# Looking up chosen key indices by rank: the one-hot table laid out with slots outermost, then ranks, heads innermost

## The chip, the cores and the metric

One Trainium2 chip, one core. The time is that of one execution on the device, in microseconds; of several runs the median counts. Before the change it is 2786.63 us (three runs, 2783.54 to 2786.88).

## The reference, cut to what matters

Two layers over 256 latent tokens and 256 context tokens of width 1024. Each layer ends in a channel mixer with 16384 experts, which are chosen by product keys: per token and head (8 heads), the query's halves are scored against two sets of 128 keys, the best 16 of each set are kept, their 256 pairs are scored by the sum, and the best 16 pairs name the experts.

```python
s = jnp.einsum('thpd,hpnd->thpn', q, keys).astype(jnp.float32)
s_top, i_top = lax.top_k(s, PEER_TOPK)
cand = (s_top[:, :, 0, :, None] + s_top[:, :, 1, None, :]).reshape(...)
cid = (i_top[:, :, 0, :, None] * PEER_NKEYS + i_top[:, :, 1, None, :]).reshape(...)
best, pos = lax.top_k(cand, PEER_TOPK)
eid = jnp.take_along_axis(cid, pos, axis=-1)
```

Layer 0 routes latent and context tokens (512), layer 1 the latent tokens alone (256). What the change touches is the last step: from a position among the candidates to the two key indices of the pair.

## The kernel before, in words

Tokens lie on the 128 partitions, in tiles i = 0, 1 of each stream (a stream is the latent or the context tokens). peer_route goes over the heads n = 0 to 7. TensorE projects the queries of a head (L796 to L798, each weight split into a rounded and a remainder part, the remainder by POOL in L153, `wl`) and scores them against the keys (L807); ACT copies the scores to SBUF (`S`, L809); DVE takes the best 16 by top16, which makes five calls: the eight largest, their indices, their replacement, the next eight, their indices (L715 to L719). Values go to `m`, indices to `ix`, both laid out [token tile, head, half a of the key, rank]. After every fourth head, for each stream, route_heads(r) is called for the heads `hs` of that half r: two streams by two halves in layer 0, one by two in layer 1, six calls in all.

route_heads copies the half's indices to bf16 (`ixb`, ACT, L726), lets POOL build 112 candidate sums per head (L729, L732), and takes the best 16 of them by top16 on DVE (`best`, `pos`). A position is turned into the ranks of its two halves by shifts and masks (L741 to L744, int32), a copy to bf16 by ACT (L746) and a few small operations on DVE (L747 to L753). Then, for each half a, a pass looks up the key index that stands at this rank:

```python
oh = wk([128, 128, 16], "oh", BF16)
nc.vector.tensor_tensor(oh, rk[:, a, :, None].to_broadcast([128, 128, 16]),
                        C["iota16"][:, None, :].to_broadcast([128, 128, 16]), op=OP.is_equal)
```

compares the 128 ranks of a token (2 tiles by 4 heads by 16 slots) with 0 to 15 (L756); two products, one per token tile, put the 16 indices in place of the ones (L760); three adds halve the 16 columns to two (L762: 1024, 512, 256 elements), and a final add of 128 elements writes the index as f32 to `i12` (L764). The gate is a softmax of `best` (L767 to L772). All of this stands on DVE unless another engine is named.

After the routing, slots_T transposes the indices and gates of each token tile on PE (`trp`, L168) into slots (L822 to L824). From them dense_experts builds a dense gate matrix in blocks of 16 tokens: DVE makes one-hot rows and weighs them (L920, L921, L925, L926; 2048 f16 elements each), PE joins them (`g_ps`, L933), ACT copies the result out and a DMA stores it. PE, ACT and POOL meanwhile work ahead on the first experts: ACT rounds the weights (`uh`, L152), POOL makes the remainders (`ul`, L153), PE multiplies (`u_ps`, L885 to L887). Then the main loop over all 128 experts runs, mostly on PE.

The order of instructions in the routing is not written by hand: the program that builds the kernel puts each engine's instructions in an order of its own, fixed before the run, and independent work (top16 of other heads, work ahead on experts) is interleaved with a pass. Only the one-hot blocks and the main loop are held in a written order.

Of the kernel before, what the change touches and what calls it, by code (L numbers as in the profile page):

```python
# [10 lines left out]
BF16 = mybir.dt.bfloat16  # L11
F16 = mybir.dt.float16
I32 = mybir.dt.int32
U32 = mybir.dt.uint32
AF = mybir.ActivationFunctionType
OP = mybir.AluOpType
# [24 lines left out]
def backbone(ctx: ExitStack, tc: tile.TileContext, x, cx, ccT, ada_w, ada_b, ada_rows, n1g, n2g, ev_in, ev_out,  # L41
             gq, gk, rlr, od_in, od_out, dlam, dsub, w_q, keysT, u_tab, v_tab, u_t, fin_g,
             ident_h, rope_c, rope_s, rel_h, iota128_h, idec_h, out):
    nc = tc.nc
# [29 lines left out]
    def wk(shape, tag, dt=F32, bufs=None):  # L74
        return P["work"].tile(shape, dt, tag=tag, name=tag, bufs=bufs)
# [47 lines left out]
    C = {}  # L123

    def late(w):

        def get(name, shape, src):
            C[name] = load(name, shape, src, nc.sync)

        with tc.issue_after(w.ins):  # L130
            C["rel"] = t2([128, 4, 128], "rel")
            nc.sync.dma_start(C["rel"], rel_h)
            C["idec"] = t2([128, 2, 128], "idec")
            nc.sync.dma_start(C["idec"], bcast(idec_h, 256))
            get("lg", [128, 2, 4], bcast(rlr, 8))
            get("ropeC", [128, 2, 64], rope_c.rearrange("(i p) d -> p i d", p=128))
            get("ropeS", [128, 2, 64], rope_s.rearrange("(i p) d -> p i d", p=128))
            get("gq", [128, 64], bcast(gq, 64))
            get("gk", [128, 64], bcast(gk, 64))
            get("subg", [128, 128], bcast(dsub, 128))  # L140
            get("iota128", [128, 128], bcast(iota128_h, 128))
        nc.vector.tensor_scalar(C["subg"], C["subg"], 1.0 - LAM_INIT, None, op0=OP.mult)
        C["iota16"] = const.tile([128, 16], BF16, name="iota16")
        nc.vector.tensor_copy(C["iota16"], C["iota128"][:, 0:16])


    def rstd(out_t, ss, n, width):
# [573 lines left out]
    def route_heads(r, m, ix, ixb, i12, gate):  # L721

        hs = slice(4 * r, 4 * r + 4)
        nc.scalar.copy(ixb[:, :, hs], ix[:, :, hs])  # L726
        cand = wk([128, 2, 4, 112], "cand")
        for i in range(2):
            nc.gpsimd.tensor_tensor(cand[:, i, :, 0:64].rearrange("p h (a b) -> p h a b", a=4),  # L729
                                    m[:, i, hs, 0, 0:4, None].to_broadcast([128, 4, 4, 16]),  # L730
                                    m[:, i, hs, 1, None, :].to_broadcast([128, 4, 4, 16]), op=OP.add)
            nc.gpsimd.tensor_tensor(cand[:, i, :, 64:112].rearrange("p h (a b) -> p h a b", a=12),  # L732
                                    m[:, i, hs, 0, 4:16, None].to_broadcast([128, 4, 12, 4]),
                                    m[:, i, hs, 1, None, 0:4].to_broadcast([128, 4, 12, 4]), op=OP.add)
        best, pos = wk([128, 2, 4, 16], "best"), wk([128, 2, 4, 16], "pos", U32)
        for i in range(2):
            for h in range(4):
                top16(best[:, i, h, :], pos[:, i, h, :], cand[:, i, h, :])
        pi = pos.rearrange("p i h k -> p (i h k)").bitcast(I32)
        ab = wk([128, 2, 2, 128], "ab", I32)  # L740
        nc.vector.tensor_scalar(ab[:, 0, 0, :], pi, 4, None, op0=OP.arith_shift_right)  # L741
        nc.vector.tensor_scalar(ab[:, 1, 0, :], pi, 15, None, op0=OP.bitwise_and)
        nc.vector.tensor_scalar(ab[:, 0, 1, :], pi, 2, None, op0=OP.arith_shift_right)
        nc.vector.tensor_scalar(ab[:, 1, 1, :], pi, 3, None, op0=OP.bitwise_and)  # L744
        abf = wk([128, 2, 2, 128], "abf", BF16)
        nc.scalar.copy(abf, ab)  # L746
        nc.vector.tensor_scalar(abf[:, 0, 1, :], abf[:, 0, 1, :], -12.0, None, op0=OP.add)  # L747
        far = wk([128, 128], "far", BF16)
        nc.vector.tensor_scalar(far, abf[:, 0, 0, :], 3.5, None, op0=OP.is_gt)
        rk = wk([128, 2, 128], "rk", BF16)  # L750
        nc.vector.tensor_sub(rk, abf[:, :, 1, :], abf[:, :, 0, :])
        nc.vector.tensor_mul(rk, rk, far[:, None, :].to_broadcast([128, 2, 128]))
        nc.vector.tensor_add(rk, rk, abf[:, :, 0, :])  # L753
        for a in range(2):
            oh = wk([128, 128, 16], "oh", BF16)
            nc.vector.tensor_tensor(oh, rk[:, a, :, None].to_broadcast([128, 128, 16]),  # L756
                                    C["iota16"][:, None, :].to_broadcast([128, 128, 16]), op=OP.is_equal)
            for i in range(2):
                o4 = oh[:, i * 64:(i + 1) * 64].rearrange("p (h k) n -> p h k n", h=4)
                nc.vector.tensor_mul(o4, o4, ixb[:, i, hs, a, None, :].to_broadcast([128, 4, 16, 16]))  # L760
            for w in (8, 4, 2):
                nc.vector.tensor_add(oh[:, :, 0:w], oh[:, :, 0:w], oh[:, :, w:2 * w])  # L762
            o3 = oh.rearrange("p (i k) n -> p i k n", i=2)
            nc.vector.tensor_add(i12[:, a, :, r * 64:(r + 1) * 64], o3[:, :, :, 0], o3[:, :, :, 1])  # L764
        g = wk([128, 8, 16], "gate_e")
        b3 = best.rearrange("p i h k -> p (i h) k")
        nc.vector.tensor_sub(g, b3, b3[:, :, 0:1].to_broadcast([128, 8, 16]))  # L767
        nc.scalar.activation(g, g, AF.Exp)
        gs = sm([128, 8], "gs")
        nc.vector.tensor_reduce(gs, g, axis=AX.X, op=OP.add)  # L770
        nc.vector.reciprocal(gs, gs)
        nc.gpsimd.tensor_mul(gate[:, :, r * 64:(r + 1) * 64].rearrange("p i (h k) -> p i h k", h=4), g.rearrange("p (i h) k -> p i h k", i=2),  # L772
                             gs.rearrange("p (i h) -> p i h", i=2)[:, :, :, None].to_broadcast([128, 2, 4, 16]))

    def peer_route(l, hi, lo, streams, order, done):


        n_t = len(streams) * T
        R = {}
        for s in streams:  # L780
            R[s] = (wk([128, 2, 8, 2, 16], f"m{s}"), wk([128, 2, 8, 2, 16], f"ix{s}", U32), wk([128, 2, 8, 2, 16], f"ixb{s}", BF16),
                    wk([128, 2, 2, 128], f"i12{s}"), P["gate"].tile([128, 2, 128], F32, tag=f"gate{s}", name=f"gate{s}"))
        for n in range(8):
            kt = wk([128, 2, 128], "kt", bufs=2)
            nc.scalar.dma_start(kt, keysT[l, :, 2 * n:2 * n + 2, :])
            Q = [mm([128, n_t], "q_ps") for _ in range(2)]
            for kk in range(4):
                eng = nc.vector if l and n < 3 and kk % 2 else nc.gpsimd
                w = P["wp"].tile([128, 2, 256], F32, tag="w", name="w", bufs=NWQ)
                nc.sync.dma_start(w, w_q[l, n, :, 2 * kk:2 * kk + 2, :])  # L790
                whi, wlo = split(*(P["wp"].tile([128, 2, 256], F32R, tag=t, name=t, bufs=NWS[l]) for t in ("wh", "wl")), w, eng)
                for a in range(2):
                    for k in range(2):
                        wh, wl = whi[:, k, a * 128:(a + 1) * 128], wlo[:, k, a * 128:(a + 1) * 128]
                        hh, hl = hi[:, 2 * kk + k, 0:n_t], lo[:, 2 * kk + k, 0:n_t]
                        nc.tensor.matmul(Q[a], wh, hh, start=kk + k == 0, stop=False)  # L796
                        nc.tensor.matmul(Q[a], wh, hl, start=False, stop=False)
                        nc.tensor.matmul(Q[a], wl, hh, start=False, stop=kk * 2 + k == KD - 1)  # L798
            qT = t4([128, 2, n_t], "qT")
            for a in range(2):  # L800
                nc.scalar.copy(qT[:, a], Q[a])
            for j, s in enumerate(streams):
                p = tr([128, 2, 2, 128], "k_ps")
                for i in range(2):
                    c = order[s][i] * 128
                    for a in range(2):
                        nc.tensor.matmul(p[:, i, a, :], qT[:, a, c:c + 128], kt[:, a, :], start=True, stop=True)  # L807
                S = wk([128, 2, 2, 128], "S", bufs=3)
                nc.scalar.copy(S, p)  # L809
                for i in range(2):  # L810
                    for a in range(2):
                        top16(R[s][0][:, i, n, a, :], R[s][1][:, i, n, a, :], S[:, i, a, :])
            if n % 4 == 3:
                for s in streams:
                    route_heads(n // 4, *R[s])
                    done(s, n // 4, R[s][3], R[s][4])
        return {s: R[s][3:] for s in streams}
# [400 lines left out]
```

## Time and profile before

| | us |
|---|---|
| median of 3 runs | 2786.63 |
| the profiled execution | 2792.03 |
| its span, first to last instruction | 2790.2 |
| PE busy | 2577.1 (92%) |
| DVE busy | 2054.8 (74%) |
| ACT busy | 1123.7 (40%) |
| POOL busy | 1025.9 (37%) |
| share of PE, DVE and POOL in the chain that ended last | 64%, 16%, 5% |

Busy times add up the instructions of an engine. A busy PE is not PE at its peak. The chain that ended last is followed back from the last instruction, at each step to what released it. In the chain, a piece is the part of an instruction that the end waited for, so it is a little shorter than the instruction's duration, since the next one starts before the last is quite through. The windows view gives busy times in a stretch; the granted clock is a share of the full TensorE clock.

### The profile page before, as it was taken

To read this page: it belongs to the slowest core of one execution; us is meant where nothing else is said; L and a number is where in the kernel's file an instruction comes from. 1 tells how busy PE (TensorE), PEld (TensorE's weight loads), DVE (VectorE), ACT (ScalarE), POOL (GpSimd) and SP (SyncE) were. 2 spreads that over 40 slices of the span, in tenths; PEclk is the share of its full clock that TensorE was granted. 3 is DMA by queue.
4 is the path that set the end of the run, shared out by engine and by line. 5 is a ranking of instruction groups with operands and counts; after the bars stand their busy time and mean duration, and the time that the engine had idled before them with its cause. 6 is when DMAs were issued, how large, how long until landed. Compare 5 with 4: busy or idle time off the path is not lost.

```text
span 2790.2 us, 39677 instructions
## 1 busy us (share of the span) xinstructions
PE 2577.1 (92%) x14787; PEld 2235.2 (80%) x14787; DVE 2054.8 (74%) x3722; ACT 1123.7 (40%) x1826; POOL 1025.9 (37%) x674
## 2 busy tenths in 40 slices
PE   7899999799799999999999998898768999999996
PEld 4776778798688888988889876676768998989984
DVE  3534589998567776777667768776994788888886
ACT  3244533354333333333333334235334455555543
POOL 0201144421567767776766401002523222222220
PEclk9999999898899999999999998999879999999998
DMA  7562422254888888888888766453336999999985
GB/s 274 179 218 83 157 91 64 82 206 201 293 291 302 284 292 279 297 299 291 295 299 307 265 206 211 163 175 101 124 131 248 319 345 332 350 335 343 340 315 186
DMA packets 263554, 667.81 MB, mean 239 GB/s; under 512 B 21760, under 2 KB 108544, under 8 KB 258752
## 3 DMA queue, kind: packets, MB, share of 16 engines
q1 hardware_dynamic: 204176, 458.81, 48.6%
q0 software_dynamic: 55296, 201.35, 20.2%
q10 hardware_dynamic: 3888, 5.11, 0.5%
q8 instruction: 116, 1.90, 0.3%
q14 instruction: 78, 0.64, 0.1%
HBM read 621.88 MB, written 42.47 MB: 238 GB/s over the span
## 4 chain that ended last, share of the span: by engine, by line
PE 64%; DVE 16%; DMA 6%; issue 6%; POOL 5%; ACT 2%; ACTq 0%; POOLq 0%; SPq 0%; DVEq 0%
PE y L985 22%; PE u_ps L887 8%; PE u_ps L886 8%; PE u_ps L885 8%; PE g_ps L933 3%; POOL row L836 3%; DMA vr<-in_v_tab_dram 3%; PE z_ps L316 2%; PE z_ps L317 2%; PE z_ps L315 2%; POOL ul L153 2%; PE trp L168 1%; DMA w<-in_ada_w_dram 1%; DVE oh L756 1%; PE mod_ps L208 1%
## 5 line engine op out<-in xcount | busy, mean ns | idle before, releaser
L985 PE MATMUL y<-vh,ww 128*128 128x512 f32 x2304 | 664.1, 398 | 26.5 <-ACT ww L966 25.8
L885 PE MATMUL u_ps<-hi,uh 128*128 128x384 f32 (+1 forms) x2048 | 636.7, 311 | 21.0 <-ACT act L892 20.7
L887 PE MATMUL u_ps<-hi,ul 128*128 128x384 f32 (+1 forms) x2048 | 638.7, 312 | 15.9 <-POOL ul L153 13.5
L886 PE MATMUL u_ps<-lo,uh 128*128 128x384 f32 (+1 forms) x2048 | 637.2, 311 | 0.0
L153 POOL TENSOR_TENSOR ul<-ur,uh 128x1024 fp32r<-128x1024 f32 x147 | 392.3, 2670 | 442.8 <-ACT uh L152 399.5
L985 PEld LDWEIGHTS y<-vh,ww 128*128 128x128 f32 x2304 | 426.4, 190 | 116.8 <-ACT ww L966 32.0
L152 ACT CAST vh<-vr 128x1024 fp32r<-128x1024 f32 x256 | 269.0, 1051 | 571.0 <-PE y L985 483.2
L153 DVE TENSOR_TENSOR vl<-vr,vh 128x1024 fp32r<-128x1024 f32 x256 | 313.4, 1224 | 152.6 <-ACT vh L152 142.5
L885 PEld LDWEIGHTS u_ps<-hi,uh 128*128 128x128 f32 x2048 | 397.1, 194 | 32.2 <-ACT act L892 21.7
L887 PEld LDWEIGHTS u_ps<-hi,ul 128*128 128x128 f32 x2048 | 396.8, 194 | 22.3 <-POOL ul L153 19.0
L985 PE MATMUL y<-vl,ww 128*128 128x512 f32 x1280 | 405.5, 398 | 2.2 <-DVE vl L153 1.9
L886 PEld LDWEIGHTS u_ps<-lo,uh 128*128 128x128 f32 x2048 | 397.1, 194 | 10.0 <-issue 1.2
L842 DVE SCALAR_TENSOR_TENSOR row<-row,h 128x1024 f32<-128x1024 f32 x192 | 290.7, 1528 | 130.2 <-DMA row<-in_u_tab_dram,eid 129.9
L848 DVE SCALAR_TENSOR_TENSOR f<-row,coef,f 128x1024 f32<-128x1024 f32 x190 | 289.8, 1525 | 105.7 <-DMA row<-in_v_tab_dram,eid 104.1
L836 POOL DMA_INDIRECT row<-in_v_tab_dram,eid x192 | 240.4, 1252 | 299.3 <-DVE w L962 188.0
L836 POOL DMA_INDIRECT row<-in_u_tab_dram,eid x192 | 240.8, 1254 | 290.2 <-DVE w L962 187.1
L152 ACT CAST uh<-ur 128x1024 fp32r<-128x1024 f32 x256 | 268.4, 1048 | 82.7 <-issue 38.7
L985 PEld LDWEIGHTS y<-vl,ww 128*128 128x128 f32 x1280 | 240.5, 189 | 64.9 <-DVE vl L153 9.8
L966 ACT CAST ww<-w 128x384 fp32r<-128x384 f32 (+1 forms) x256 | 110.2, 431 | 221.8 <-DVE w L962 219.7
L149 POOL TENSOR_TENSOR rs<-rs,nhalf 128x4 f32<-128x4 f32 (+2 forms) x19 | 22.4, 1177 | 458.7 <-DVE rs L148 349.6
L152 ACT CAST wh<-w 128x512 fp32r<-128x512 f32 (+2 forms) x136 | 109.6, 810 | 196.9 <-PE z_ps L317 69.7
L892 ACT ACTIVATE act<-u_ps 128x384 f32<-128x384 f32 (+1 forms) x256 | 104.8, 409 | 164.6 <-PE u_ps L887 162.5
(270 smaller groups left out, 3836.6 us busy)
## 6 DMA issues: line engine op xcount, KB each, us to landing
ur<-in_u_t_dram SPq DMA_DIRECT2D x256, 512.0 KB
vr<-in_v_tab_dram SPq DMA_DIRECT2D x256, 512.0 KB
w<-in_ada_w_dram SPq DMA_DIRECT2D x96, 512.0 KB
gd<-stage SPq DMA_DIRECT2D x36, 1024.0 KB
G<-gd SPq DMA_DIRECT2D x16, 1536.0 KB
w<-in_w_q_dram SPq DMA_DIRECT2D x64, 256.0 KB
w<-in_od_in_dram SPq DMA_DIRECT2D x24, 512.0 KB
G<-gd SPq DMA_DIRECT2D x16, 768.0 KB
```

Source lines behind the costliest of these rows:

```text
L152: nc.scalar.copy(hi, src)
L153: (eng or nc.vector).tensor_tensor(lo, src, hi.bitcast(F32), op=OP.subtract)
L836: nc.gpsimd.indirect_dma_start(out=r[n], out_offset=None, in_=v_tab if n >= S else u_tab, in_offset=bass.IndirectOffsetOnAxis(ap=eid[:, n ...
L842: nc.vector.scalar_tensor_tensor(t, t, 1.0, h2, op0=OP.mult, op1=OP.mult, accum_out=coef[:, n:n + 1])
L848: nc.vector.scalar_tensor_tensor(f, t, coef[:, j:j + 1], f, op0=OP.mult, op1=OP.add)
L885: nc.tensor.matmul(p, uh[:, k, :], hi[:, k, 0:ntok], start=k == 0, stop=False)
L886: nc.tensor.matmul(p, uh[:, k, :], lo[:, k, 0:ntok], start=False, stop=False)
L887: nc.tensor.matmul(p, ul[:, k, :], hi[:, k, 0:ntok], start=False, stop=k == KD - 1)
L892: nc.scalar.activation(act[e], ps.pop(e), AF.Gelu)
L933: nc.tensor.matmul(v["p"][t // 4][:, t % 4, :], o2[:, t // 4, :, t % 4], o1[:, t // 4, :, t % 4], start=n == 0, stop=n == 1)
L966: nc.scalar.copy(ww[:, 0:ntok], w)
L985: nc.tensor.matmul(y[j][:, d, :], x1, x2[:, d * 512:(d + 1) * 512], start=e == 0 and n == 0, stop=e == 127 and n == len(sums) - 1)
```

## The change

The table `oh` of a pass gets the order slots, ranks, heads in place of (heads, slots), ranks: 16 slots by 16 ranks by 8 heads (2 token tiles by 4 heads). The ranks `rk`, the positions read for them, and the bf16 indices `ixb` get the heads innermost; the row of 0 to 15 becomes a table of 16 ranks by 8 heads. The two products become one, the final add becomes two, and the copy of indices becomes two, one per half a. `ixb` now holds the heads of one half of the calls only, and is written again by the second.

```diff
--- before.py
+++ after.py
@@ -140,8 +140,8 @@
             get("subg", [128, 128], bcast(dsub, 128))
             get("iota128", [128, 128], bcast(iota128_h, 128))
         nc.vector.tensor_scalar(C["subg"], C["subg"], 1.0 - LAM_INIT, None, op0=OP.mult)
-        C["iota16"] = const.tile([128, 16], BF16, name="iota16")
-        nc.vector.tensor_copy(C["iota16"], C["iota128"][:, 0:16])
+        C["ranks"] = const.tile([128, 16, 8], BF16, name="ranks")
+        nc.vector.tensor_copy(C["ranks"], C["iota128"][:, 0:16, None].to_broadcast([128, 16, 8]))
 
 
     def rstd(out_t, ss, n, width):
@@ -723,7 +723,8 @@
 
 
         hs = slice(4 * r, 4 * r + 4)
-        nc.scalar.copy(ixb[:, :, hs], ix[:, :, hs])
+        for a in range(2):
+            nc.scalar.copy(ixb[:, a].rearrange("p n (i h) -> p i h n", i=2), ix[:, :, hs, a, :])
         cand = wk([128, 2, 4, 112], "cand")
         for i in range(2):
             nc.gpsimd.tensor_tensor(cand[:, i, :, 0:64].rearrange("p h (a b) -> p h a b", a=4),
@@ -736,32 +737,32 @@
         for i in range(2):
             for h in range(4):
                 top16(best[:, i, h, :], pos[:, i, h, :], cand[:, i, h, :])
-        pi = pos.rearrange("p i h k -> p (i h k)").bitcast(I32)
-        ab = wk([128, 2, 2, 128], "ab", I32)
-        nc.vector.tensor_scalar(ab[:, 0, 0, :], pi, 4, None, op0=OP.arith_shift_right)
-        nc.vector.tensor_scalar(ab[:, 1, 0, :], pi, 15, None, op0=OP.bitwise_and)
-        nc.vector.tensor_scalar(ab[:, 0, 1, :], pi, 2, None, op0=OP.arith_shift_right)
-        nc.vector.tensor_scalar(ab[:, 1, 1, :], pi, 3, None, op0=OP.bitwise_and)
+        pi = pos.rearrange("p i h k -> p k (i h)").bitcast(I32)
+        ab = wk([128, 2, 2, 16, 8], "ab", I32)
+        nc.vector.tensor_scalar(ab[:, 0, 0], pi, 4, None, op0=OP.arith_shift_right)
+        nc.vector.tensor_scalar(ab[:, 1, 0], pi, 15, None, op0=OP.bitwise_and)
+        nc.vector.tensor_scalar(ab[:, 0, 1], pi, 2, None, op0=OP.arith_shift_right)
+        nc.vector.tensor_scalar(ab[:, 1, 1], pi, 3, None, op0=OP.bitwise_and)
         abf = wk([128, 2, 2, 128], "abf", BF16)
-        nc.scalar.copy(abf, ab)
+        nc.scalar.copy(abf, ab.rearrange("p a f k n -> p a f (k n)"))
         nc.vector.tensor_scalar(abf[:, 0, 1, :], abf[:, 0, 1, :], -12.0, None, op0=OP.add)
         far = wk([128, 128], "far", BF16)
         nc.vector.tensor_scalar(far, abf[:, 0, 0, :], 3.5, None, op0=OP.is_gt)
-        rk = wk([128, 2, 128], "rk", BF16)
-        nc.vector.tensor_sub(rk, abf[:, :, 1, :], abf[:, :, 0, :])
-        nc.vector.tensor_mul(rk, rk, far[:, None, :].to_broadcast([128, 2, 128]))
-        nc.vector.tensor_add(rk, rk, abf[:, :, 0, :])
+        rk = wk([128, 2, 16, 8], "rk", BF16)
+        rf = rk.rearrange("p a k n -> p a (k n)")
+        nc.vector.tensor_sub(rf, abf[:, :, 1, :], abf[:, :, 0, :])
+        nc.vector.tensor_mul(rf, rf, far[:, None, :].to_broadcast([128, 2, 128]))
+        nc.vector.tensor_add(rf, rf, abf[:, :, 0, :])
         for a in range(2):
-            oh = wk([128, 128, 16], "oh", BF16)
-            nc.vector.tensor_tensor(oh, rk[:, a, :, None].to_broadcast([128, 128, 16]),
-                                    C["iota16"][:, None, :].to_broadcast([128, 128, 16]), op=OP.is_equal)
-            for i in range(2):
-                o4 = oh[:, i * 64:(i + 1) * 64].rearrange("p (h k) n -> p h k n", h=4)
-                nc.vector.tensor_mul(o4, o4, ixb[:, i, hs, a, None, :].to_broadcast([128, 4, 16, 16]))
+            oh = wk([128, 16, 16, 8], "oh", BF16)
+            nc.vector.tensor_tensor(oh, rk[:, a, :, None, :].to_broadcast([128, 16, 16, 8]),
+                                    C["ranks"][:, None].to_broadcast([128, 16, 16, 8]), op=OP.is_equal)
+            nc.vector.tensor_mul(oh, oh, ixb[:, a, None].to_broadcast([128, 16, 16, 8]))
             for w in (8, 4, 2):
                 nc.vector.tensor_add(oh[:, :, 0:w], oh[:, :, 0:w], oh[:, :, w:2 * w])
-            o3 = oh.rearrange("p (i k) n -> p i k n", i=2)
-            nc.vector.tensor_add(i12[:, a, :, r * 64:(r + 1) * 64], o3[:, :, :, 0], o3[:, :, :, 1])
+            for i in range(2):
+                nc.vector.tensor_add(i12[:, a, i, r * 64:(r + 1) * 64].rearrange("p (h k) -> p k h", h=4),
+                                     oh[:, :, 0, i * 4:i * 4 + 4], oh[:, :, 1, i * 4:i * 4 + 4])
         g = wk([128, 8, 16], "gate_e")
         b3 = best.rearrange("p i h k -> p (i h) k")
         nc.vector.tensor_sub(g, b3, b3[:, :, 0:1].to_broadcast([128, 8, 16]))
@@ -778,7 +779,7 @@
         n_t = len(streams) * T
         R = {}
         for s in streams:
-            R[s] = (wk([128, 2, 8, 2, 16], f"m{s}"), wk([128, 2, 8, 2, 16], f"ix{s}", U32), wk([128, 2, 8, 2, 16], f"ixb{s}", BF16),
+            R[s] = (wk([128, 2, 8, 2, 16], f"m{s}"), wk([128, 2, 8, 2, 16], f"ix{s}", U32), wk([128, 2, 16, 8], f"ixb{s}", BF16),
                     wk([128, 2, 2, 128], f"i12{s}"), P["gate"].tile([128, 2, 128], F32, tag=f"gate{s}", name=f"gate{s}"))
         for n in range(8):
             kt = wk([128, 2, 128], "kt", bufs=2)
```

## Rows read from the trace of the kernel before

**Rows 1.** Windows: start:end, us, busy PE, PEld, DVE, ACT, POOL (instructions), clock, DMA share, GB/s
```profile
410.00:440.00 30.00, 24.91 (x101) 19.89 (x102) 30.00 (x109) 7.08 (x13) 13.83 (x11) 0.85 0.23 75
...
650.00:700.00 50.00, 44.21 (x346) 41.58 (x344) 40.55 (x33) 23.73 (x40) 2.24 (x2) 0.83 0.46 190
...
2000.00:2020.00 20.00, 10.41 (x73) 10.07 (x72) 20.00 (x116) 4.09 (x5) 3.89 (x4) 0.78 0.10 27
...
2080.00:2100.00 20.00, 17.98 (x149) 17.58 (x147) 19.73 (x16) 10.63 (x18) 2.94 (x1) 0.84 0.48 184
```

**Rows 2.** Chain that ended last: start us, us, what; where the look-up ends
```profile
548.19 0.40 DVE i L764
...
548.64 0.69 PE trp L168 x2
...
2048.35 1.11 PE trp L168 x4
```

**Rows 3.** Waits, 380 to 560 us, then 1980 to 2125: total us, times, longest
```profile
PE trp L168 <- DVE i L764: 11.8, 4, 6.1
...
PE trp L168 <- DVE i L764: 19.2, 2, 15.2
```

**Rows 4.** Chain, one undisturbed pass of the look-up in layer 0
```profile
447.96 2.19 DVE oh L756
...
450.42 1.19 DVE oh L760 x2
...
451.88 0.60 DVE oh L762
...
452.68 0.32 DVE oh L762
...
453.28 0.29 DVE oh L762
...
453.76 0.29 DVE i L764
```

**Rows 5.** Chain, the one-hot stage of layer 0
```profile
676.69 1.15 DVE ol L921
...
677.86 1.24 DVE oh L925
```

**Rows 6.** Timeline of DVE, small operations: start us, us, line, operation
```profile
434.86 0.27 DVE L767 TENSOR_TENSOR gate_e<-best 128x128 f32<-128x128 f32 x1
435.05 0.22 DVE L741 TENSOR_SCALAR ab<-pos 128x128 int32<-128x128 int32 x1
435.18 0.22 DVE L742 TENSOR_SCALAR ab<-pos 128x128 int32<-128x128 int32 x1
...
439.24 0.27 DVE L753 TENSOR_TENSOR rk<-rk,abf 128x256 bf16<-128x256 bf16 x1
```

**Rows 7.** Timeline of ACT, layer 0, second half
```profile
482.63 0.41 ACT L726 CAST ixb<-ix 128x256 bf16<-128x256 uint32 x1 [3.05 <-DVE ix L719]
```

**Rows 8.** Groups by form on DVE (| busy us, mean ns |), 405 to 549, then 1984 to 2050
```profile
L756 DVE TENSOR_TENSOR oh<-rk,iota 128x2048 bf16<-128x2048 bf16 x8 | 20.2, 2529 | 0.1
L760 DVE TENSOR_TENSOR oh<-oh,ixb 128x1024 bf16<-128x1024 bf16 x16 | 16.6, 1078 | 0.1
...
L762 DVE TENSOR_TENSOR oh<-oh 128x256 bf16<-128x256 bf16 x8 | 9.1, 1134 | 0.1
...
L762 DVE TENSOR_TENSOR oh<-oh 128x1024 bf16<-128x1024 bf16 x8 | 8.0, 1004 | 0.1
...
L760 DVE TENSOR_TENSOR oh<-oh,ixb 128x1024 bf16<-128x1024 bf16 x8 | 7.1, 921 | 0.1
L762 DVE TENSOR_TENSOR oh<-oh 128x1024 bf16<-128x1024 bf16 x4 | 4.9, 1223 | 0.1
```

**Rows 9.** Timelines from 528 us, DVE, then POOL
```profile
531.10 5.49 DVE L760 TENSOR_TENSOR oh<-oh,ixb 128x1024 bf16<-128x1024 bf16 x2
...
530.25 5.78 POOL L153 TENSOR_TENSOR ul<-ur,uh 128x1024 fp32r<-128x1024 f32 x2 [1.99 <-ACT uh L152]
```

## The prediction

> **What bounds the kernel now.** I read the page first: 2790.2 us of span, PE busy 92% of it, so on the average this is a TensorE kernel. The look-up that the change touches runs on DVE, though, so I went to the windows view for the two stretches in which it runs. In layer 0 DVE is busy in all 30.00 us of the window from 410 us, while PE is busy in 24.91; in layer 1 it is busy in all 20.00 us from 2000 us, with PE at 10.41 [rows 1]. In these stretches DVE is the engine that everything waits for. The chain of waits says the same in order of time: it runs from one DVE instruction to the next through the last pass of the look-up, whose final add starts at 548.19 us, and steps from there to the transposes of PE (548.64) that turn the found indices into slots; from the second layer the chain has the same step at 2048.35 [rows 2]. The table of waits gives it from PE's side: PE's transposes waited 11.8 us for the look-up's last add (L764) in layer 0, 6.1 of it at once, and 19.2 us in layer 1 [rows 3]. So time saved on DVE here should move the end, if nothing else is nearly as late.
>
> It is passed on, too. Behind the slots come the one-hot blocks (L920 to L926): in layer 1 DVE is busy 19.73 of 20.00 us there, and in layer 0 PE takes over for part of the stage (DVE 40.55 of 50 and PE 44.21 in the window from 650 us) [rows 1]. PE's work there is a fixed amount behind the same transposes, so an earlier start shifts it as long as PE had been waiting.
>
> **The change part by part.** route_heads is called six times (two streams by two halves in layer 0, one by two in layer 1), and its loop over a makes 12 passes.
>
> A pass that nothing disturbs costs, in pieces of the chain, 2.19 for the compare (L756), 1.19 for the two products (L760), 0.60, 0.32 and 0.29 for the three adds of the tree (L762) and 0.29 for the final add (L764): 4.88 us [rows 4].
>
> The compare has 2048 bf16 elements and takes one operand with every element repeated 16 times innermost. Nearly the same instruction stands in the one-hot stage: L921 compares 2048 f16 elements whose repeated operand has its repetition in the middle and runs of 4 innermost, and takes 1.15 us; the product L925 takes 1.24 [rows 5]. The changed compare has runs of 8 innermost and the repetition in the middle, so I take 1.15. The two products become one of 2048 elements; I take 1.24 (two of 1024 cost 1.19 now, so it gains nothing). The first two adds keep their elements and lie in longer runs: 0.60 and 0.32 as now. The third, now in runs of 2, comes to lie in one run of 16 per slot. L753, 256 bf16 elements in one run, lasts 0.27; an L767 that also lasts 0.27 is followed 0.19 us later by the next instruction [rows 6], so I take 0.19. The final add becomes two of 64 elements each, which read runs of 4 and write with a stride of 64 bytes. No row shows this form: the lower end is the 0.13 between two shifts of 128 elements [rows 6], the upper end the 0.29 of today's strided final add [rows 4]. I take 0.20 each, near the 0.19 of a plain two-input instruction (L767). New pass: 1.15 + 1.24 + 0.60 + 0.32 + 0.19 + 0.40 = 3.90, a saving of 0.98 (0.80 to 1.12). **12 passes: -11.8 us (-9.6 to -13.4).**
>
> The four shifts and masks (L741 to L744) now read the positions with a stride of 64 bytes. The same 128 elements are converted, so a gain is excluded; the price of strides in this trace is that L764 costs 0.29 where the contiguous L767 costs 0.19 for as many elements, 0.10. I take half: 24 instructions by 0.05 = **+1.2 us (0 to +2.4)**, all on DVE's path.
>
> On ACT one copy of indices to bf16 (0.41 us) becomes two of half the size, at most 0.41 more in six places. ACT stood idle 3.05 us before it, waiting for DVE's last index [rows 7], and the product that reads it comes after the whole choice of candidates. It gets one new wait: the table now holds one half's heads, so the second half's copy may not start before the first half's last product. That product is issued before the second half's eight rounds of top-16, so it is long done. Queued behind the copy on ACT are casts of weights and the gelus; if the wait did hold, they would be late by the rest of that product, 1.24 us at most. I count nothing. The rank table of 128 elements is made once and far from here: nothing. No DMA and no queue changes.
>
> The third term is stalls. Against the undisturbed pieces (plus the 0.08 by which a duration exceeds a piece), the sums by form show: in layer 0 L756 20.2 for 18.2, L760 16.6 for 10.8, the smallest add 9.1 for 3.0, the largest 8.0 for 5.4; in layer 1 L760 7.1 for 5.4 and the largest add 4.9 for 2.7 [rows 8]. Together some 20 us, 1.7 per pass. What DVE waits for is seen in one place: a pair of products that should take 1.19 took 5.49 while POOL ran two splits of weights, 5.78 us from 530.25 [rows 9]. If stalls go with the length of a pass, they fall by a fifth (3.90 to 4.88): -4.1; if with the number of splits, by nothing. I take **-2.1**.
>
> [...]
>
> **Sum:** -11.8 + 1.2 - 2.1 = -12.7 us; I say -13. The profiled execution took 2792.0 us (span 2790.2 and 1.8 around it) and would take 2779; it is 5.4 over the median of 2786.6, from which I forecast **2773.6**. PE ran at a granted clock of 0.85 and 0.78 in the windows in which it waits [rows 1]; shorter waits may give a little of that back, which I leave to the range.
>
> **The rivals.**
> 1. *PE takes over in layer 0.* The eight passes there give two thirds of the sum, about 8.5 us. PE's waits for L764 are 11.8 us in that stretch [rows 3], which is enough to take it up; against it, PE also waits for POOL's splits, which do not come earlier by themselves. If half is lost: -9, 2778.
> 2. *More than forecast.* Stalls fall with the passes, the final adds cost 0.13, and PE's waits shrink with its clock higher: -13.4 - 4.1 - 2 = -20, 2767.
> 3. *POOL's splits eat it (the other side).* Place: DVE's queue, in the passes. [...] Price: the worst pair lost 4.3 us in one pass [rows 9], 2.6 above today's mean. Without a change in stalls the gain is 10.6, so 0.9 more of stall per pass cancels it, and it is slower by over 0.2% (5.6 us) from 1.35 more per pass, at some 3.1 instead of 1.7. At 3.5 the time is 2786.6 - 10.6 + 12 x 1.8 = 2798. For it: nearly every slow instruction today has a POOL split beside it. Against it: the splits are as many as before, and already cost DVE much of their length.
> 4. *The change doesn't do what it says*: the compare stays at 2.19 because its repeated middle dimension isn't taken at the faster rate. Then a pass costs 4.94, the shifts 1.2: +2, 2789. L921 speaks against it.
> 5. [...] If the 64-byte strides of the positions and of the final adds cost a full access per element, the new forms pay on 24 x 128 + 24 x 64 = 4608 elements; 3.5 ns on each would be 16 us and make it slower by 0.2%. L764 today shows 0.10 us on 128 elements, 0.8 ns. At 4 ns: 2786.6 - 12.7 + 18 = 2792. [...]
>
> The builder may also write another order of instructions for DVE and PE; one wait as that of the first transposes, 6.1 us [rows 3], more or less is what I allow for this.
>
> **How the numbers follow.** Forecast (2769 to 2778) 0.47; rival 1 (2778 to 2781) 0.17; rival 2 (2760 to 2769) 0.17; rival 3 0.13, of which 0.05 slower by more than 0.2% and 0.08 between 2781 and 2792; rival 4 0.03; rival 5 0.03. 0.2%, 5.6 us, is about what a measurement of this kernel can tell from no change. Faster: 0.47 + 0.17 + 0.17 and 0.01 of rival 3, 0.82; within: 0.07 + 0.03 = 0.10; slower: 0.08. The range of 2761 to 2783 leaves out most of rivals 3 to 5 and the tail of rival 2.
>
> **What would show it.** The compare should last 1.2 us instead of 2.27, the one product as much, two final adds near 0.28, the shifts under 0.32; the sums of these groups tell work from stalls. The transposes of slots should come some 8 us earlier in layer 0 and 13 in layer 1, and the gap stay to the end. Wrong would be: a compare still at 2.2; a longer idle time of DVE waiting for g_ps behind the transposes (rival 1); sums of L760 and L762 that grow (rival 3); or transposes that come earlier with an unchanged end.

## The result, and the profile after

Eight runs of each kernel on one chip: 2768.89 us after (2762.21 to 2775.99), 2791.9 before (2783.54 to 2799.22). The ratio is 0.9917, with a 95% interval of 0.9896 to 0.9938: **23 us faster (17 to 29)**, where 12.7 were forecast. The profiled execution took 2764.36 us, its span 2762.6.

The pieces of the changed pass where nothing disturbs them, in the chain of waits of the kernel after (start us, us, what; the two final adds stand as one row, x2, here from another pass):

```profile
499.08 1.12 DVE oh L758
...
507.20 1.12 DVE oh L760
...
508.58 0.59 DVE oh L762
...
509.42 0.33 DVE oh L762
...
509.94 0.19 DVE oh L762
```

```profile
450.03 0.30 DVE i L764 x2
```

The compare, 2.19 before [rows 4], takes 1.12; the pass is 1.12 + 1.12 + 0.59 + 0.33 + 0.19 + 0.30 = 3.65 instead of 4.88. The two final adds together cost what the one did (0.29). The shifts, which now read with a stride of 64 bytes, follow each other by 0.17 us instead of 0.13 [rows 6] (timeline of DVE, kernel after):

```profile
433.02 0.25 DVE L742 TENSOR_SCALAR ab<-pos 128x128 int32<-128x128 int32 x1
433.19 0.26 DVE L743 TENSOR_SCALAR ab<-pos 128x128 int32<-128x128 int32 x1
```

The groups by form on DVE answer to [rows 8]; first layer 0 (405 to 537 us), then layer 1 (1955 to 2022 us). Columns: busy us, mean ns of one, idle before.

```profile
L760 DVE TENSOR_TENSOR oh<-oh,ixb 128x2048 bf16<-128x2048 bf16 x8 | 13.5, 1688 | 0.1
L758 DVE TENSOR_TENSOR oh<-rk,ranks 128x2048 bf16<-128x2048 bf16 x8 | 9.7, 1209 | 0.1
L762 DVE TENSOR_TENSOR oh<-oh 128x1024 bf16<-128x1024 bf16 x8 | 8.3, 1038 | 0.1
L764 DVE TENSOR_TENSOR i<-oh 128x64 f32<-128x64 bf16 x16 | 6.1, 440 | 0.1
L762 DVE TENSOR_TENSOR oh<-oh 128x256 bf16<-128x256 bf16 x8 | 5.0, 621 | 0.1
L762 DVE TENSOR_TENSOR oh<-oh 128x512 bf16<-128x512 bf16 x8 | 4.1, 511 | 0.1
...
L758 DVE TENSOR_TENSOR oh<-rk,ranks 128x2048 bf16<-128x2048 bf16 x4 | 5.7, 1424 | 0.1
L760 DVE TENSOR_TENSOR oh<-oh,ixb 128x2048 bf16<-128x2048 bf16 x4 | 5.7, 1421 | 0.1
L762 DVE TENSOR_TENSOR oh<-oh 128x1024 bf16<-128x1024 bf16 x4 | 3.6, 904 | 0.1
```

A mean near the undisturbed duration (1.21 us for the compare) says that nothing held the instruction up; the excess over it, times the count, is called the stall here. Over all six groups the excess is 12.7 us in layer 0 and 2.7 in layer 1. The same reckoning for the kernel before, over all its forms, gives 17.4 and 4.8: stalls fell by some 7 us. In layer 0 the compare does not stall at all any more (1209 mean, 20.2 for eight at 2529 before).

So the stretch from the first copy of positions to the last transposes of slots shrank from 140.3 to 127.1 us in layer 0, and from 62.7 to 55.0 in layer 1. What became of this is read in the chain's shares by line from there to the start of the main loop in layer 0, for the kernel before (549 to 714 us) and the kernel after (536 to 710 us):

```profile
by line: PE g_ps L933 43.8%; PE u_ps L885 10.7%; PE u_ps L886 10.7%; PE u_ps L887 10.6%; DMA G<-gd 5.1%; DVE oh L925 3.7%; DVE ol L926 3.7%; DVE o L920 3.5%; DVE ol L921 3.5%; DMA gd<-stage 3.1%; PE trp L168 0.4%; ACT stage L938 0.4%; DVE w
```

```profile
by line: PE g_ps L934 50.3%; PE u_ps L886 11.3%; PE u_ps L887 11.2%; PE u_ps L888 11.2%; DMA G<-gd 4.0%; DMA gd<-stage 3.5%; DVE ol L927 2.6%; DVE ol L922 2.1%; DVE oh L926 1.4%; DVE o L921 0.7%; PE y L986 0.5%; ACT stage L939 0.3%; DVE w L
```

DVE's four lines of the one-hot stage had 14.4% of that chain and have 6.8%; PE's `g_ps` and `u_ps` grew from 76% to 84%. The windows of the same two stretches (columns as in [rows 1]) show that PE also has more to do in the second:

```profile
549.00:714.00 165.00, 145.21 (x1058) 137.06 (x1056) 136.40 (x101) 73.13 (x121) 30.53 (x12) 0.89 0.54 202
```

```profile
536.00:710.00 174.00, 155.70 (x1124) 146.67 (x1123) 142.37 (x100) 77.80 (x127) 43.17 (x16) 0.94 0.54 202
```

The second has 66 matmuls more, 10.5 us of busy PE. All but four of them are work on experts that was moved. The windows of the tile `u_ps` alone, from the last transposes to the main loop, show it (start:end, us, busy PE with the number of matmuls, clock, DMA share, GB/s; before, then after):

```profile
549.20:714.25 165.05, 59.59 (x288) 0.89 0.54 202
```

```profile
536.50:709.65 173.15, 71.32 (x350) 0.95 0.54 202
```

Over the look-up and this stretch together, the `u_ps` matmuls take 134.8 us before and 135.0 after: the work is the same, but 62 of them, 11.7 us, stand behind the look-up now and stood in it before. This is not a matter of one execution. In all traces of the kernel before 288 stand there in PE's own order of instructions, in all of the kernel after 350: the program that builds the kernel wrote another order for PE. DVE waits for `g_ps` 8.5 us before and 11.3 after (tables of waits, 549 to 700 us):

```profile
DVE o L920 <- PE g_ps L933: 8.5, 8, 1.6
```

```profile
DVE o L921 <- PE g_ps L934: 11.3, 10, 1.7
```

From the first copy of positions to the first matmul of the main loop it was 306.0 us and is 300.6: of some 13 to 14 us, **5.4 reach the main loop in layer 0**. In layer 1 the 7.7 us are passed on whole (the one-hot stage takes 72.1 and 72.2 us). That is 13 us. The other 10 are not in the look-up; in these two executions the main loop of layer 0 is shorter, 959.5 us instead of 974.0, though the instructions of every engine stand in the same order there.

### The profile page after: what moved, and what is told of

Same layout as the page of the kernel before. It is cut to its first block, busy times and chain, and to the rows that moved or that the text cites. A ratio compares the mean times of both kernels' runs of the same rounds, so it can differ in the third digit from the quotient of the medians.

```text
span 2762.6 us, 39685 instructions
## 1 busy us (share of the span) xinstructions
PE 2570.7 (93%) x14787; PEld 2235.6 (81%) x14787; DVE 2060.6 (75%) x3722; ACT 1127.4 (41%) x1832; POOL 1021.3 (37%) x674
## 3 DMA queue, kind: packets, MB, share of 16 engines
q1 hardware_dynamic: 204176, 458.81, 48.5%
## 4 chain that ended last, share of the span: by engine, by line
PE 77%; DVE 12%; DMA 5%; issue 2%; ACT 1%; POOL 1%; SPq 0%; ACTq 0%; POOLq 0%; DVEq 0%
PE y L986 28%; PE u_ps L888 10%; PE u_ps L887 10%; PE u_ps L886 10%; PE g_ps L934 4%; PE z_ps L315 3%; PE z_ps L316 3%; PE z_ps L317 3%; DMA vr<-in_v_tab_dram 2%; PE trp L168 1%; DMA w<-in_ada_w_dram 1%; PE q_ps L799 1%; PE q_ps L798 1%; PE mod_ps L208 1%; PE q_ps L797 1%
## 5 line engine op out<-in xcount | busy, mean ns | idle before, releaser
L153 POOL TENSOR_TENSOR ul<-ur,uh 128x1024 fp32r<-128x1024 f32 x147 | 382.5, 2603 | 419.9 <-ACT uh L152 339.4
L153 DVE TENSOR_TENSOR vl<-vr,vh 128x1024 fp32r<-128x1024 f32 x256 | 313.2, 1223 | 204.0 <-ACT vh L152 197.2
L843 DVE SCALAR_TENSOR_TENSOR row<-row,h 128x1024 f32<-128x1024 f32 x192 | 297.2, 1565 | 93.9 <-DMA row<-in_u_tab_dram,eid 93.5
L837 POOL DMA_INDIRECT row<-in_u_tab_dram,eid x192 | 252.1, 1313 | 272.4 <-DVE w L963 187.1
L837 POOL DMA_INDIRECT row<-in_v_tab_dram,eid x192 | 236.4, 1231 | 300.5 <-DVE w L963 187.8
L849 DVE SCALAR_TENSOR_TENSOR f<-row,coef,f 128x1024 f32<-128x1024 f32 x190 | 304.2, 1601 | 50.4 <-DMA row<-in_v_tab_dram,eid 47.9
L153 DVE TENSOR_TENSOR ul<-ur,uh 128x1024 fp32r<-128x1024 f32 x109 | 133.1, 1221 | 26.2 <-ACT uh L152 26.2
```

Of the source, the lines that this page charges most:

```text
L153: (eng or nc.vector).tensor_tensor(lo, src, hi.bitcast(F32), op=OP.subtract)
L837: nc.gpsimd.indirect_dma_start(out=r[n], out_offset=None, in_=v_tab if n >= S else u_tab, in_offset=bass.IndirectOffsetOnAxis(ap=eid[:, n ...
L843: nc.vector.scalar_tensor_tensor(t, t, 1.0, h2, op0=OP.mult, op1=OP.mult, accum_out=coef[:, n:n + 1])
L849: nc.vector.scalar_tensor_tensor(f, t, coef[:, j:j + 1], f, op0=OP.mult, op1=OP.add)
```

## The experiments

Twelve runs, on three chips, each beside runs of the kernel before on the same chip (medians 2790.35, 2791.45, 2788.61). "Below" is the ratio to them, with its interval, in us of that median.

**The two kernels again** (no edit).

> The kernel before, unchanged, for a second trace. In the first pair of traces the main loop of layer 0 (first product into y to the first gate product behind it) took 979 us before and 965 after, in the same order of instructions. If this is scatter between executions, this loop comes out anywhere between 964 and 980; if it belongs to the kernel, at 977 to 981. Time against before: 0, within 0.2%.

> The changed kernel, unchanged, for a second trace. Scatter: its main loop of layer 0 lies anywhere between 964 and 980 us. A property of the kernel: 963 to 967. Time against before: 15 to 29 us less. The last transposes of layer 0 at 536 us again and the first product into y at 710.

Measured: 2792.19 (ratio 1.0003, 0.9987 to 1.0019) and 2769.31 (0.9918, 0.9894 to 0.9941). The 23 us repeat. The look-up stretch of layer 0 is 141.2 and 126.0 us, that of layer 1 62.6 and 54.9: each repeats within about 1 us. The stage before the look-up and the main loop of layer 0 scatter by several us from one execution to the next (986.1 and 962.3 here), so single executions can't say whose loop is shorter. The loop is counted here from the first product into `y` to the first gate product behind it; by this count the 979 and 965 us of the expectations are 974.0 and 959.5. The 986.1 lies outside both ranges that had been set for it.

**The new layout in one layer alone.** The other layer calls the function of before, and both tables are kept.

```diff
-                    route_heads(n // 4, *R[s])
+                    (route_heads if l == 0 else route_heads_rows)(n // 4, *R[s])
```

> New layout in layer 0 alone (8 of 12 passes). Theory A, what DVE saves reaches the end in full: the stretch of the look-up was 14.6 us shorter in the trace, so -13 to -16 us. Theory B, PE takes over in the one-hot stage and leaves 4.6, but the loop is shorter for good: -4.6 - 14 = -15 to -19. Theory C, PE takes over and the shorter loop was scatter: -3 to -6.

> New layout in layer 1 alone (4 of 12 passes). Its look-up was 7.7 us shorter in the trace, and DVE sets the stage behind it. Theories A and B: -7 to -9 us. Theory C: the rest of the 23 us has to come from here, -12 to -18. Its layer 0 is that of before: main loop of 977 to 981 us if its length belongs to the kernel.

Measured: layer 0 alone 2782.19 (0.9973, 0.9955 to 0.9991), 7.5 us below; layer 1 alone 2782.53 (0.9980, 0.9960 to 1.0000), 5.6 below. The stretches are as short as with both (126.1 and 55.0 us), and in layer 0 it is again 300.5 us to the main loop: one layer's look-up does not need the other's. But 7.5 + 5.6 = 13, not 23. Neither lies in a range that had been set: nearest are theory C for layer 0 (3 to 6) and theories A and B for layer 1 (7 to 9). Both were run once more:

> The new layout in layer 0 alone, a second time: is its share of the gain the -7.5 us of the first time, and is the main loop of layer 0 again shorter (964.7 us then, against 974.0 and 986.1 in two executions of the kernel before)? Theory A (layer 0 passes on only what TensorE had waited for): the start of the main loop is 6 us earlier, the loop's length scatters by about 10 us in either kernel, the median is 6 to 9 us below the kernel before. Theory B (the order that the builder gives the one-hot stage of layer 0 makes the loop shorter for good): the loop lasts 960 to 966 again, and the median is 12 to 18 us below.

> The new layout in layer 1 alone, a second time. Theory A: the look-up stretch of layer 1 is 7.7 us shorter (55.0 us) and passed on in full, the median 7 to 9 us below the kernel before; the main loop of layer 0, which has the order of before, lasts 965 to 986. Theory B: median again 5 to 8 below, and the loop of layer 0 is 970 or more in every execution of this order.

Measured: 2785.87 (0.9984, 0.9964 to 1.0005), 4.5 below, and 2782.21 (0.9979, 0.9958 to 1.0000), 5.9 below. The loop of layer 0 took 980.6 us in the one and 959.5 in the other, the wrong way round for an order that shortens the loop for good: theory B of both falls. Theory A's rule of what is passed on stands, its medians (6 to 9 below) were a little high. About 12 us below for the two, twice.

**The compare slowed again.** The table of ranks in f32 is the only edit. The built order of PE changes with it: 303 `u_ps` matmuls stand behind the last transposes of layer 0, not 350.

```diff
-        C["ranks"] = const.tile([128, 16, 8], BF16, name="ranks")
+        C["ranks"] = const.tile([128, 16, 8], F32, name="ranks")
```

> The changed kernel with its table of ranks kept in f32 and not bf16, and nothing else: the compare then has one f32 operand, and should fall back to about 2.2 us a piece (+1.06 in each of 12 passes), while product, tree and final adds stay as they are. Theory A (the compare's rate is the saving, stalls go with the length of a pass): the compare lasts 2.2 to 2.3 us; the stretch from the first copy of positions to the last transposes of slots grows by 8 x 1.06 = 8.5 us in layer 0 (126.5 to about 135) plus some 4 us of stalls that come back, to 139; in layer 1 by 4.2 plus 1 to 2, from 55 to about 61; the end is 8 to 14 us later than the changed kernel, at 2777 to 2783. Theory B (the new forms save by running into fewer splits of POOL whatever the compare lasts): the stalls stay at today's 12.6 and 2.7 us, the stretches reach 135 and 59 and the end is 6 to 9 us later. Theory C (the end is moved by the order of the main loop of layer 0, not by the look-up): the stretches grow, the end stays within 4 us of the changed kernel.

The group by form on DVE in layer 0 (410 to 557 us):

```profile
L758 DVE TENSOR_TENSOR oh<-rk,ranks 128x2048 bf16<-128x2048 bf16 x8 | 20.2, 2521 | 0.1
```

The eight compares take what they took before the change, and their stalls are back; the stretches are 138.6 and 61.3 us, as theory A had it (139 and 61), and the main loop of layer 0 starts 306.0 us behind the first positions, as before the change. The end too is where A put it, at 2779.6. So **nearly all that the look-up saves hangs on the compare's rate**: directly, by fewer stalls, and by the order that the builder writes with it. How much of the rest is stalls and how much is order, this run does not tell. But this kernel, whose look-up is within 4 us of the old one, is still 10 us below the kernel before (0.9964, 0.9947 to 0.9981). Whatever gives the second half of the gain survives without the first.

**Where the tiles start.** What the slow compare shares with the changed kernel, and the one-layer kernels with the kernel before, is an address. The old row of ranks takes 32 bytes per partition, the new table 256 (512 in f32); the one-layer kernels keep both, 288. Tiles are placed one behind the other, so nearly every buffer behind the table (weights, gathered rows, the rings of the main loop) starts 32 bytes past a multiple of 128 in the kernel before and the one-layer kernels, and on a multiple of 128 in the others. Two kernels shift them and leave every instruction as it is:

```diff
-        C["iota16"] = const.tile([128, 16], BF16, name="iota16")
+        C["iota16"] = const.tile([128, 32], BF16, name="iota16")[:, 0:16]
```

> The kernel before with its row of 0 to 15 kept in a tile of 64 bytes instead of 32 (the other half unused): not one instruction differs, but every tile that is placed behind it moves up by 32 bytes, so that weights, gathered rows and loop buffers start on multiples of 64 bytes as they do in the changed kernel, where they start 32 bytes past one in the kernel before and in the two kernels with the new layout in one layer only. Theory A (where the tiles start is worth the part of the gain that the look-up does not explain): the hardware queue's packets take 1.2% less time (some 1338 us of the 16 engines' span instead of 1354), TensorE waits less for POOL's splits in the main loop of layer 0, and the end is 6 to 12 us earlier: 2779 to 2785 beside 2791. Theory B (the starts do not matter, the two halves of the change help each other through the order in which the builder writes them): within 3 us of the kernel before.

```diff
-        C["ranks"] = const.tile([128, 16, 8], BF16, name="ranks")
+        C["ranks"] = const.tile([128, 18, 8], BF16, name="ranks")[:, 0:16]
```

> The changed kernel with 32 unused bytes behind its table of ranks: not one instruction differs, but the tiles behind it start 32 bytes past a multiple of 64 again, as before the change. Theory A: the look-up stretches stay at 126.5 and 55.0 us, the packets of the hardware queue take some 1354 us instead of 1338, and the end is 6 to 12 us later than the changed kernel, at 2776 to 2782: about the 13 us that the two stretches pass on (6 of layer 0, 7.7 of layer 1) below the kernel before. Theory B: no difference from the changed kernel, 2766 to 2772.

> The changed kernel as it is, beside the three others of this call. Both theories: 2766 to 2772, 23 us below the kernel before.

Measured: the shifted changed kernel 2777.84 (0.9957, 0.9937 to 0.9978), 12.0 us below the kernel before, beside the changed kernel with 2765.86 (0.9917, 0.9885 to 0.9948), 23 below. **32 unused bytes cost 12 us**; the look-up is the same, 127.0 and 55.0 us, and the products stall as much (group by form on DVE, layer 0, 407 to 540 us):

```profile
L760 DVE TENSOR_TENSOR oh<-oh,ixb 128x2048 bf16<-128x2048 bf16 x8 | 13.5, 1686 | 0.1
```

In the traces every engine of the shifted kernel has its instructions in the order of the changed one. The runs of the two themselves differ by 11.5 us in the mean, with an interval of 6 to 17.

But the kernel before with 32 bytes more stayed at 2788.93 (1.0005, 0.9982 to 1.0028): there theory A falls as I had put it. Its tiles start on multiples of 64, yet 64 bytes past a multiple of 128. The share of the hardware queue in the 16 engines' span tells it from the changed kernel, which moves the same bytes; here the DMA rows (queue, kind: packets, MB, share) of the kernel before as run in the first experiment, before moved by 32, after shifted by 32, and after, run a third time:

```profile
q1 hardware_dynamic: 204176, 458.81, 48.4%
```

```profile
q1 hardware_dynamic: 204176, 458.81, 48.5%
```

```profile
q1 hardware_dynamic: 204176, 458.81, 48.8%
```

```profile
q1 hardware_dynamic: 204176, 458.81, 48.3%
```

Times their spans (2798.9, 2794.8, 2775.2 and 2766.8 us) this is 1355, 1355, 1354 and 1336 us. Over all fourteen profiled executions:

| where the tiles start | executions | packets of the hardware queue, us | of these, the packets of 512 bytes, us | main loop of layer 0, us, mean |
|---|---|---|---|---|
| 32 past a multiple of 128 | before, before again, the four one-layer, after shifted | 1348 to 1356 | 138.1 to 139.0 | 959.5 to 986.1, 971.9 |
| 64 past one | before moved by 32 | 1355 | 138.0 | 974.5 |
| on one | after (three), slow compare, one pass (two) | 1336 to 1343 | 127.5 to 128.9 | 959.5 to 966.5, 963.1 |

The two ranges of packet times don't meet, and the loop's mean differs by 9 us. Sorted by size (durations of the packets in each trace, summed and divided by the 16 engines), most of the difference lies in the packets of 512 bytes: 73984 in each trace, 29.8 to 30.1 ns each off a multiple of 128 and 27.6 to 27.9 on one. All packets of other sizes together take 1210 to 1219 us and 1208 to 1216, and these ranges overlap. 73728 of the 512-byte packets are the loads of the gate matrix into `G` (DMA issues of the page, kernel after):

```profile
G<-gd SPq DMA_DIRECT2D x16, 1536.0 KB
...
G<-gd SPq DMA_DIRECT2D x16, 768.0 KB
```

The program places `G` 32 bytes past a multiple of 256 in the first group, 64 past one in the kernel before moved by 32, and on a multiple of 256 in the last group. So moving the kernel before by 32 left these packets as slow as they were, as it left the time. Inside the loop, PE waits for POOL's splits of the weights: 14.4 us in the kernel before, run again, and 1.5 in the changed kernel, run a third time (tables of waits, 725 to 1670 us):

```profile
PE u_ps L887 <- POOL ul L153: 14.4, 15, 2.8
```

```profile
PE u_ps L888 <- POOL ul L153: 1.5, 3, 0.7
```

These waits scatter widely (0 to 14.4 us over the executions off a multiple of 128, 0.6 to 4.1 on one). A packet of 512 bytes takes 27.7 ns where `G` starts on a multiple of 256 and 30.0 off one. The packets of 4096 bytes show no such step (932 to 941 us off, 931 to 939 on). **Shown** is that a shift of 32 bytes costs the changed kernel 12 us, and that it slows the loads of `G` by 10 us of queue time (128.6 to 139.0). That the one comes of the other, and through POOL's splits, is not shown: layer 1 alone, run again, has the slow packets and yet a loop of 959.5 us without any such wait. The kernel before was not tried on a multiple of 128, nor the changed kernel 64 past one. The nearest to the first is the slow compare, whose tiles start on one and which is 10 us below the kernel before with almost the old look-up. The mechanism stays open.

**Both halves in one pass.** One compare and one product of 4096 elements, the tree on [128, 32, 16, 8].

```diff
-        for a in range(2):
-            oh = wk([128, 16, 16, 8], "oh", BF16)
...
+        oh = wk([128, 2, 16, 16, 8], "oh", BF16)
+        o3 = oh.rearrange("p a k r n -> p (a k) r n")
+        nc.vector.tensor_tensor(o3, rk.rearrange("p a k n -> p (a k) n")[:, :, None, :].to_broadcast([128, 32, 16, 8]),
+                                C["ranks"][:, None].to_broadcast([128, 32, 16, 8]), op=OP.is_equal)
```

> The changed kernel with both halves a in one pass: one compare and one product of 4096 elements, three adds of twice the size, four final adds as before. Per call 5 instructions fewer, each worth the fixed part of an instruction (about 0.06 to 0.08 us: 1.13 for 2048 elements at 0.52 ns each leaves 0.06). Theory A (the gain is work on DVE): 6 x 0.35 = 2 us less on DVE's path, of which half is given back in layer 0: 1 to 2 us faster than the changed kernel, not to be told from it by time, but the stretches shorten by 1.5 and 0.7 us. Theory B (stalls are set by the number of two-input instructions that meet a split of POOL): five instructions fewer per call leave fewer places to stall in, the stall sums fall by a third, 4 to 6 us: 3 to 6 us faster. Theory C (a longer instruction is met by a split all the same, and holds POOL longer in turn): stalls unchanged or larger, 0 to 4 us slower.

> The changed kernel with both halves a in one pass, a second time, now beside the changed kernel itself. Its look-up stretch in layer 0 was 124.8 us instead of 126.5 and that of layer 1 as long. Theory A (a saving of some 2 us of work): 0 to 3 us below the changed kernel, too little to be told. Theory B (the 5.3 us by which the two medians of two calls differed is real): 4 to 7 us below it, at 2761 to 2765.

Measured: 2763.63 (0.9917, 0.9892 to 0.9942) and 2763.83 (0.9907, 0.9877 to 0.9936), the latter beside 2765.86 for the changed kernel: 2 us lower, which this measurement can't tell from nothing. The stretch of layer 0 is 124.8 and 124.5 us, that of layer 1 unchanged. The stalls of layer 0 did fall by about a third, as theory B had it (some 13 us by the shortest duration of each form in the changed kernel, 8.7 and 8.4 here), but little of it shows in the stretch and none that can be told in the time. It is faster than the kernel before, and not shown to be faster than the changed one. The 0.52 ns per element of the expectation agrees with the undisturbed pieces of the changed kernel, 1.12 us for 2048 elements and 0.59 for 1024.

## Why the prediction was right, and where it was not

The time of 2768.9 lies in the range of 2761 to 2783, and the sign was right, for the reason given: DVE bounds the look-up, the compare there is slow by its form (2.19 us, 1.12 in the new one), and the end follows. How near the time came to the forecast of 2773.6 is in part luck: the gain was 23 us (17 to 29) and not 13, some 10 of it from a source that the prediction did not have, and the forecast started from a three-run median of 2786.6, where eight runs give 2791.9. The 12.7 us forecast for the look-up are even close to what the shifted kernel shows it to be worth, 12.0 (6.1 to 17.6). But that agreement is made of terms that missed in opposite directions.

- **The pass** was mis-sized: 1.23 us saved, not 0.98. The compare took 1.12 where 1.15 was taken, the product 1.12 where 1.24 was taken from L925, and the final adds 0.30 where 0.40 was; 12 passes give 14.8 us, past the upper bound of 13.4. The two adds share one row's 0.30 although each was set near 0.20.
- **The shifts** cost 0.04 each, 1.0 us; 0.05 was taken.
- **Stalls** fell by some 7 us, not 2.1. "If with the number of splits, by nothing" was the wrong end: when the compare is slowed again, the stalls of the look-up rise by about 4 us. In the timelines of DVE and POOL every instruction of the passes that lasts over 0.2 us longer than the shortest of its form has a split (L153) beside it, 16 before and 13 after; but of the eight faster compares of layer 0 three have one beside them too, and none of the eight is held up (1209 ns mean, 1226 the longest).
- **Handing on in layer 0** is the step that failed: "PE's work there is a fixed amount behind the same transposes". It is not: PE works ahead on experts during the look-up, and with the shorter look-up the builder's order leaves 62 more of these matmuls, 11.7 us, to be done behind it. The forecast had two thirds of the sum from layer 0; 5 to 6 us of some 14 arrive. This is rival 1 at more than the half I gave it, and the sign named for it, a longer wait of DVE for `g_ps`, is there. The prediction did allow for another order of PE, but as one wait of 6.1 us more or less. The transposes were expected some 8 us earlier in layer 0; they came 12.4 earlier (536.2 instead of 548.6 us), and most of that was given back before the main loop began. In layer 1 they came 29.1 earlier (2019.7 instead of 2048.8), where 13 were expected.
- **"No DMA and no queue changes"** is the other. The transfers do not change, but the start of what they write does, and with it some 10 us. No rival held this; rival 2, whose 2767 is near the result, would have got there through stalls, final adds and the clock, which is not how it came about.
- **Rivals 3, 4 and 5** fell: the sums of the products and the tree did not grow (13.5 and 17.4 us in layer 0, 16.6 and 20.5 before), the compare runs at the faster rate, and a stride of 64 bytes cost 0.04 us on 128 elements, 0.3 ns each. The 3.5 ns set there as the price of "slower by 0.2%" is a slip: 4608 elements at 3.5 ns are 16.1 us, 3.4 above the gain of 12.7; the 5.6 us of 0.2% need 4.0 ns.

## What to carry to other kernels

Where VectorE compares against a repeated operand, put the repetition in a middle dimension and leave real elements innermost: here this halved the instruction (2.19 us to 1.12 for 2048 bf16 elements). Where another engine works ahead while a stage is waited for, ask how much of that work the wait had hidden: when the wait shrinks, it stands behind it (here 62 matmuls, 11.7 us). And when a change alters the size of a small table, test it with padding that leaves all instructions as they are, before the whole difference is put down to the instructions, and sort the DMA packets of both traces by size.

## What had not been expected of the hardware

32 unused bytes per partition moved a 2766 us kernel by 12 us, with no instruction changed; the same number of bytes moved the kernel before by 0.3 us. The packets of one DMA queue, for the same 204176 packets and 458.81 MB, took 1336 to 1343 us in the executions whose tiles start on multiples of 128 bytes and 1348 to 1356 in the others. Most of the difference, some 10 us, is that of the 512-byte packets that fill one buffer, `G`: 27.7 ns each where it starts on a multiple of 256 bytes, 30.0 where it starts 32 or 64 past one.
